# A list scheduler's time model: measured matmul distances and a port lock between VectorE and GpSimd

## The chip, the core and the metric

The kernel runs on one core of one Trainium2 chip. A core has a matrix engine (TensorE, "PE" in the profile; its weight loads are shown as "PEld"), a vector engine (VectorE, "DVE"), an activation engine (ScalarE, "ACT"), a general engine (GpSimd, "POOL") and SyncE ("SP"), whose queue issues all DMAs of this kernel. Each engine works through its own queue in the order in which the program put the instructions there, and waits at an instruction until the semaphores that it needs are set. The metric is the device time of one execution in microseconds, as the median of several runs.

## What is computed

Two layers of a streaming encoder on 2048 frames of width 1024, in float32. Each layer has a gated linear attention (4 heads, chunks of 64) and a differential softmax attention (4 heads, two maps each), one input projection and one output projection:

```
for l in range(DEPTH):
    mod = c_act @ w_ada[l] + b_ada[l]
    shift, scale, gate = jnp.split(mod, 3, axis=-1)
    h = rms_norm(x, norm_g[l]) * (1.0 + scale[:, None]) + shift[:, None]
    proj = h @ w_in[l]
    gq, gk, gv, glr, gz, dq, dk, dv, dz = split_columns(proj)
    gqkv = jax.nn.silu(causal_depthwise_conv(jnp.concatenate([gq, gk, gv], axis=-1), conv_w[l]))
    ...
    o_gla = gla_branch(gq, gk, gv, glr, gz, w_gk[l], b_gk[l], gla_norm_g[l])
    ...
    o_diff = diff_branch(dq, dk, dv, dz, qn_g[l], kn_g[l], lam, lam_init, diff_norm_g[l])
    y = jnp.concatenate([o_gla, o_diff], axis=-1).astype(x.dtype) @ w_out[l]
    x = x + gate[:, None] * y
```

## The kernel before

**Tiling.** The frames are taken in 4 blocks of 512 (`UT`), for each of 2 layers. For a block, `prep_gen` loads x, normalises and transposes it to `hhi` and `hlo`, the high and low halves of h^T in a rounded float32 type (F32R). `dense_gen` runs the input projection as items of 512 columns: three matmuls of 512 columns for each pair of 128-row tiles (high x high, high x low, low x high), summed in the accumulators `acc` (4 banks of PSUM, the matmul's output memory). `gla_gen` works the linear attention (`uT`: convolved values before their transposes; `E`, `vN`: keys and values; `Sn`: states). `head_evac` and `qk_gen` bring one softmax head's queries and keys to `qh`, `ql` and `Kt` (`rq`: a reciprocal root, made by GpSimd's pow; `qk`: rows scaled by it). `attn_gen` takes a head in 4 query tiles: scores into `sc`, VectorE's running minimum into `s`, ScalarE's exp, VectorE's combination of the two maps with the factor `r`, transposes into `tp`, a copy `aT` by ScalarE, and the product with V into `po`; `z` is the gated result, `oT` its transpose. `out_gen` splits `oT` into `oh` and `ol` and runs the output projection.

**Weights.** `weights` (line 552) loads a weight tile. At the first block of a layer (u = 0) it loads the raw tile, ScalarE rounds the high half, GpSimd subtracts for the low half (line 562), and both are written to DRAM (`wd`); the later blocks load the split tile from there. GpSimd's subtractions are therefore all in the first block's pass of each layer, and in the output projection's first pass of each layer.

**What sets the order.** The generators run as streams and record every operation in `Program.ops`, with its dependences and a cost in ns (`cost`). Then `order` plays the program: it keeps for each engine the time at which it is free, for each operation the time at which its inputs and its buffer are there (with fixed latencies `LAT` between engines), and picks again and again the engine that can start first, giving it, of the operations that are ready, the one recorded first. Matmuls count double where the modelled clock is cold. The result is one list, and `issue` (line 277) emits the instructions in that order, so that it fixes each engine's queue, SP's with the DMAs among them. All instructions come from one line of `issue`, which is why the profile puts L284 on every group; groups are told apart by their tiles. On the chip, semaphores hold the order of dependences; the modelled times have no effect there.

**Lines that matter.** `cost`, line 160: for TensorE a fixed 110 ns for a transpose; for a matmul n columns over a rate, with a lower bound from the 107 ns of a weight load or from 216 ns, plus 3. For GpSimd 300 + 165 n ns for pow and 100 + 2.2 n otherwise. For VectorE 0.52 ns a column for copies and `tensor_scalar` on SBUF operands (SBUF is the on-chip memory of the engines), 1.042 otherwise, plus fixed parts. `order`: line 243 takes the ready operation, the last `else` (line 258) advances the free time of VectorE, GpSimd and, outside of table loads, ScalarE.

Of the kernel before, what the change touches and what calls it, by code (L numbers as in the profile page):

```python
# [20 lines left out]
P = 128  # L21
# [4 lines left out]
CH = 64  # L26
# [91 lines left out]
class Program:  # L118
# [40 lines left out]
    @staticmethod  # L159
    def cost(e, method, args, kw, out):  # L160
        n = math.prod(out.shape[1:])
        if e == "S":
            return math.prod(out.shape) * 4 / 360.0
        if e == "T":
            if method == "transpose":
                return 110
            rate = {F32R: 2.4, BF16: 2.4, F32: 0.6}[args[2].dt]
            if rate == 0.6 and args[1].shape[1] < P:
                return max(n / rate * args[1].shape[1] / P, 78)
            return max(n / rate, 107 * args[1].shape[1] / P if rate == 2.4 else 216) + 3  # L170
        ins = [a for a in list(args[1:]) + list(kw.values()) if isinstance(a, View) and a is not kw.get("accum_out")]
        scalars = sum(math.prod(a.shape[1:]) == 1 for a in ins) if n > 1 else 0
        psum = any(a.buf.psum for a in ins)
        if method == "tensor_reduce":
            n = math.prod(ins[0].shape[1:])
        if e == "A":
            return 0.834 * n + (52 if psum else 93) + 93 * (scalars + ("accum_out" in kw))
        if e == "G":
            return 300 + 165 * n if kw.get("op") == ALU.pow else 100 + 2.2 * n
        fast = method in ("tensor_copy", "tensor_scalar") and not psum  # L180
        return (0.52 if fast else 1.042) * n + 68 + 61 * scalars

    @staticmethod
    def table(op):
# [3 lines left out]
    def order(self):  # L188
        ops, N = self.ops, len(self.ops)
        left, uses, turn = {}, [], {}  # L190
        for o in ops:
            for b in o[6]:
                if b not in left:
                    left[b] = 0
                    turn.setdefault((b.pool, b.tag), []).append(b)
                left[b] += 1
        place = {b: k for q in turn.values() for k, b in enumerate(q)}
        nxt = dict.fromkeys(turn, 0)
        slots = {t: [{} for _ in range(q[0].bufs or q[0].pool.bufs)] for t, q in turn.items()}
        blocked = {t: [] for t in turn}  # L200
        slot, used = {}, {}
        succ = [[] for _ in range(N)]
        nd = [len(o[4]) for o in ops]
        for i, o in enumerate(ops):
            for j in o[4]:
                succ[j].append(i)
        ready = [0.0] * N
        free = dict.fromkeys(self.engines, 0.0)
        dma = 0.0
        pend = {e: [] for e in free}  # L210
        avail = {e: [] for e in free}
        todo = [i for i in range(N) if nd[i] == 0]
        table, flight = None, [-1e4] * 8
        work, win = {}, 3413
        res = []
        while len(res) < N:
            while todo:
                now, todo = sorted(todo), []
                for i in now:
                    e, bufs = ops[i][0], ops[i][6]  # L220
                    for b in bufs:
                        t = (b.pool, b.tag)
                        if b not in slot and (place[b] != nxt[t] or not slots[t]):
                            blocked[t].append(i)
                            break
                    else:
                        for b in bufs:
                            if b not in slot:
                                t = (b.pool, b.tag)
                                slot[b] = min(slots[t], key=lambda u: max(u.values(), default=0.0))  # L230
                                slots[t].remove(slot[b])
                                used[b] = {}
                                nxt[t] += 1
                                todo += blocked[t]
                                blocked[t] = []
                            for e2, x in slot[b].items():
                                ready[i] = max(ready[i], x + (self.LAT[e2][e] if e != e2 or e == "S" else 0))
                        heapq.heappush(pend[e], (ready[i], i))
            t, e = min((free[e] if avail[e] else max(free[e], pend[e][0][0]), e)
                       for e in free if avail[e] or pend[e])  # L240
            while pend[e] and pend[e][0][0] <= t:
                heapq.heappush(avail[e], heapq.heappop(pend[e])[1])
            i = heapq.heappop(avail[e])
            if e == "S":
                free[e] = t + 475
                dma = end = max(dma, t + 1150, flight[-8] + 2000) + ops[i][5]
                flight.append(end)
            elif e == "A" and self.table(ops[i]) not in (None, table):
                table = self.table(ops[i])
                free[e] = end = t + ops[i][5] + 1283  # L250
            elif e == "T":
                w = int(t / win)
                warm = work.get(w - 1, 0.0) > 0.5 * win
                free[e] = end = t + ops[i][5] * (1 if warm else 2)
                if ops[i][1] == "transpose" or ops[i][2][2].shape[-1] > 1:
                    for v in range(w, int(end / win) + 1):
                        work[v] = work.get(v, 0.0) + min(end, (v + 1) * win) - max(t, v * win)
            else:
                free[e] = end = t + ops[i][5]
            res.append(i)  # L260
            for j in succ[i]:
                ready[j] = max(ready[j], end + self.LAT[e][ops[j][0]])
                nd[j] -= 1
                if nd[j] == 0:
                    todo.append(j)
            for b in ops[i][6]:
                used[b][e] = max(used[b].get(e, 0.0), end)
                left[b] -= 1
                if left[b] == 0:
                    t_ = (b.pool, b.tag)  # L270
                    slots[t_].append(used[b])
                    todo += blocked[t_]
                    blocked[t_] = []
        self.span = max(free.values()) / 1e3
        return res
# [12 lines left out]
def trunk_kernel(ctx, tc, x, c, w_ada, b_ada, norm_g, w_in, conv_w, w_gk, b_gk, gla_norm_g,  # L288
# [226 lines left out]
    def pe(cost, wait=0.0):  # L515
        return ("pe", cost, wait)
# [614 lines left out]
    def dense_stream():  # L1131
        order = (0, 4, 1, 2, 5, 3, 6)
        prev = None
        for l in range(L):
            for u in range(NU):
                yield need("h", l * NU + u, lag=2.0)
                if prev:
                    yield from out_gen(*prev)
                yield from dense_gen(l, u, (0, 4, 1, 5, 2, 3, 6) if u == 0 else order)
                prev = (l, u)  # L1140
        yield from out_gen(*prev)
# [47 lines left out]
```

## Time and profile before

| | us |
|---|---|
| median of 3 runs | 2660.28 (2659.81 to 2660.94) |
| the profiled execution | 2664.22 |
| its span, first to last instruction | 2662.5 |
| TensorE busy | 2573.6 |
| VectorE busy | 1768.3 |
| ScalarE busy | 1207.0 |
| GpSimd busy | 625.3 |

The profiled execution is a single one and has a time of its own, 1.7 us longer than its span. A row of the groups reads: line, engine, operation, output tile <- input tiles, shapes, count, then busy us, mean ns of one, then the idle time of the engine before such an instruction and who ended it. A row of the waits reads: who waited, for whom, total us, number of times, longest us. A row of a timeline reads: start us, length us, engine, line, operation, tiles, shape, count, and in brackets the idle time before it. A row of the chain that ended last reads: start us, length us, engine and tile, count. A matmul's busy time is longer than its distance to the next one, since they are pipelined.

### The profile page before, as it was taken

The numbers are of one execution on the slowest core, as the hardware profiler recorded it, in microseconds if no ns is written. First come the engines' busy times: TensorE is split into PE (matmuls) and PEld (weight loads), VectorE is DVE, ScalarE is ACT, GpSimd is POOL, SyncE is SP. The second block draws the span as 40 slices with busy tenths as digits, with TensorE's granted clock in tenths as the row PEclk, the third lists the DMA queues.
The fourth block names the chain that finished last, engine by engine and source line by source line (L and its number), as shares of the span: only waits on it lengthen the run. The fifth ranks groups of instructions, "written<-read, shape, count | busy, mean of one in ns | idle before, by whom it ended". The sixth has DMA issues, their size and how long they took to land. (4 is left out here: it accounts for less than half of the span.)

```text
span 2662.5 us, 41105 instructions
## 1 busy us (share of the span) xinstructions
PE 2573.6 (97%) x13987; PEld 2070.3 (78%) x13987; DVE 1768.3 (66%) x5104; ACT 1207.0 (45%) x2592; POOL 625.3 (23%) x852
## 2 busy tenths in 40 slices
PE   7999899999999999999999989999999999999997
PEld 4777678877888778887777767887788877888886
DVE  4778757873767837676738764667637786387764
ACT  3555524453444533444634563344614456154442
POOL 2455411121010210102154554111121111210111
PEclk9999999999999999999999999999999999999998
DMA  8766586446552465334277656443374433734242
GB/s 278 243 229 240 205 295 198 160 154 213 170 186 96 151 206 171 139 131 136 83 263 250 230 202 244 163 175 139 124 262 151 150 130 112 265 121 153 91 139 103
DMA packets 201613, 476.12 MB, mean 179 GB/s; under 512 B 20735, under 2 KB 78269, under 8 KB 201405
## 3 DMA queue, kind: packets, MB, share of 16 engines
q1 hardware_dynamic: 201404, 473.50, 52.1%
q8 instruction: 111, 1.82, 0.3%
q14 instruction: 98, 0.79, 0.1%
HBM read 362.29 MB, written 111.15 MB: 178 GB/s over the span
## 5 line engine op out<-in xcount | busy, mean ns | idle before, releaser
L284 PE MATMUL acc<-w,hhi 128*128 128x512 f32 x2560 | 844.5, 405 | 5.9 <-DMA w<-wd 2.8
L284 PEld LDWEIGHTS acc<-w,hhi 128*128 128x128 f32 x2560 | 462.5, 189 | 106.0 <-issue 13.1
L284 PE MATMUL acc<-w,hlo 128*128 128x512 f32 x1280 | 507.4, 398 | 0.0
L284 ACT ACTIVATE s<-s,mx 128x512 f32<-128x512 f32 (+15 forms) x256 | 308.0, 1204 | 342.7 <-DVE s L284 341.3
L284 PE MATMUL acc<-hhi,w 128*128 128x512 f32 x1024 | 373.6, 406 | 1.2 <-DVE z L284 0.5
L284 PE MATMUL acc<-w,oh 128*128 128x512 f32 x1024 | 335.8, 403 | 8.6 <-DVE t L284 4.7
L284 DVE TENSOR_SCALAR_CACHE_REDUCE s<-sc,mx 64x64 f32<-64x64 f32 (+5 forms) x640 | 307.5, 485 | 43.6 <-PE sc L284 25.2
L284 PEld LDWEIGHTS acc<-w,hlo 128*128 128x128 f32 x1280 | 241.2, 188 | 51.1 <-issue 2.0
L284 POOL MEMSET s<- 64x64 f32 x256 | 39.0, 154 | 1027.3 <-DVE s L284 463.7
L284 POOL TENSOR_TENSOR w<-raw,w 128x512 fp32r<-128x512 f32 x144 | 195.0, 1364 | 194.1 <-ACT w L284 171.3
L284 PEld LDWEIGHTS acc<-w,oh 128*128 128x128 f32 x1024 | 191.2, 191 | 53.7 <-DVE t L284 8.5
L284 PEld LDWEIGHTS acc<-hhi,w 128*128 128x128 f32 x1024 | 192.5, 188 | 41.7 <-issue 1.2
L284 ACT COPY aT<-tp 128x512 f32<-128x512 f32 (+2 forms) x320 | 162.7, 520 | 115.5 <-PE tp L284 111.7
L284 PE MATMUL po<-Vj,aT 128*128 128x128 f32 x1536 | 205.2, 277 | 4.9 <-ACT aT L284 4.8
L284 PE MATMUL acc<-w,ol 128*128 128x512 f32 x512 | 202.9, 400 | 0.9 <-DVE ol L284 0.7
L284 PE MATMUL acc<-hlo,w 128*128 128x512 f32 x512 | 203.0, 396 | 0.0
L284 DVE TENSOR_SCALAR_CACHE_REDUCE s<-sc 128x512 f32<-128x512 f32 (+4 forms) x256 | 158.5, 623 | 66.9 <-PE sc L284 62.5
L284 PEld LDWEIGHTS po<-Vj,aT 128*128 128x128 f32 x1536 | 191.6, 193 | 14.6 <-ACT aT L284 9.1
L284 DVE SCALAR_TENSOR_TENSOR s<-s,r 128x512 f32<-128x512 f32 (+2 forms) x320 | 200.6, 676 | 2.9
L284 DVE TENSOR_TENSOR ol<-oT,oh 128x512 fp32r<-128x512 f32 x128 | 105.2, 828 | 120.2 <-ACT oh L284 108.7
L284 PE MATMUL tp<-ident,s 128*128 128x128 f32 x1088 | 172.5, 274 | 11.8 <-DVE s L284 9.4
L284 POOL TENSOR_TENSOR rq<-qss,mhalf 128x4 f32<-128x4 f32 x128 | 128.9, 1026 | 192.8 <-DVE qss L284 192.4
(167 smaller groups left out, 4209.2 us busy)
## 6 DMA issues: line engine op xcount, KB each, us to landing
w<-wd SPq DMA_DIRECT2D x432, 512.0 KB, 3.6
wd<-w SPq DMA_DIRECT2D x144, 512.0 KB, 3.4
raw<-in_w_in_dram SPq DMA_DIRECT2D x112, 256.0 KB, 4.3
Kj<-kd SPq DMA_DIRECT2D x48, 512.0 KB, 5.0
wr<-in_w_ada_dram SPq DMA_DIRECT2D x128, 128.0 KB, 3.2
kd<-Kt SPq DMA_DIRECT2D x24, 512.0 KB, 2.8
Vj<-vd SPq DMA_DIRECT2D x48, 256.0 KB, 4.1
xt<-in_x_dram SPq DMA_DIRECT2D x16, 512.0 KB, 3.8
```

The source lines that it names most:

```text
L284: getattr(self.engines[e], method)(*[real(a) for a in args], **{k: real(v) for k, v in kw.items()})
```

## The change

Only the two functions that model time are changed, with a new one beside them; no operation is added or removed, and the buffers are the same. In `cost`, a matmul with F32R (or BF16) operands takes 0.4512 ns a column, at least 112 ns for a full weight load and with no constant; F32 matmuls get 7 ns in place of 3; narrow F32 matmuls on 64 rows take 1.4 times as long. The new `paired` says which operations use the ports that VectorE and GpSimd share: four methods, with no operand in PSUM, all of GpSimd's and those of VectorE with more than one element a row. In `order`, a time `ports` holds until when these ports are taken: an engine whose next operation is paired takes the first ready operation that isn't, if there is one; else it starts when the ports come free. GpSimd's `memset` isn't paired, its pow (a `tensor_tensor`) is, for its whole cost.

```diff
             if rate == 0.6 and args[1].shape[1] < P:
-                return max(n / rate * args[1].shape[1] / P, 78)
-            return max(n / rate, 107 * args[1].shape[1] / P if rate == 2.4 else 216) + 3
+                return max(n / rate * args[1].shape[1] / P, 78) * (1.4 if args[1].shape[0] == CH else 1)
+            if rate == 2.4:
+                return max(0.4512 * n, 112 * args[1].shape[1] / P)
+            return max(n / rate, 216) + 7
...
+    @staticmethod
+    def paired(op):
+
+        e, method, args, kw = op[:4]
+        if e not in "VG" or method not in ("tensor_tensor", "scalar_tensor_tensor", "tensor_copy", "tensor_scalar"):
+            return False
+        ins = [a for a in list(args[1:]) + list(kw.values()) if isinstance(a, View) and a is not kw.get("accum_out")]
+        return not any(a.buf.psum for a in ins) and (e == "G" or math.prod(args[0].shape[1:]) > 1)
...
+        paired, ports = [self.paired(o) for o in ops], 0.0
...
             i = heapq.heappop(avail[e])
+            if paired[i] and ports > t:
+                later = [i]
+                while paired[i] and avail[e]:
+                    i = heapq.heappop(avail[e])
+                    later.append(i)
+                if paired[i]:
+                    i = later[0]
+                    t = ports
+                later.remove(i)
+                for j in later:
+                    heapq.heappush(avail[e], j)
...
             else:
                 free[e] = end = t + ops[i][5]
+                if paired[i]:
+                    ports = end
```

## The prediction

> **What bounds the kernel now.** I read the profile's page first, then the busy time by stage, then what TensorE waited for in each stage, because the change touches nothing but the order in which the instructions stand on their queues: it can win or lose only where an engine waits.
>
> ```profile
> span 2662.5 us, 41105 instructions
> PE 2573.6 (97%) x13987; PEld 2070.3 (78%) x13987; DVE 1768.3 (66%) x5104; ACT 1207.0 (45%) x2592; POOL 625.3 (23%) x852
> ...
> 0.00:60.00 60.00, 42.22 (x276) 28.22 (x277) 26.79 (x102) 18.92 (x38) 12.51 (x22) 0.97 0.86 279
> 60.00:400.00 340.00, 314.91 (x1561) 240.93 (x1559) 242.60 (x638) 163.79 (x391) 149.29 (x162) 0.99 0.72 243
> 400.00:1330.00 930.00, 923.14 (x5194) 753.48 (x5193) 644.68 (x1914) 433.64 (x891) 147.51 (x246) 1.00 0.47 157
> 1330.00:1600.00 270.00, 251.29 (x1278) 197.84 (x1276) 183.07 (x500) 132.82 (x332) 136.90 (x152) 0.98 0.69 233
> 1600.00:1940.00 340.00, 333.79 (x1743) 264.85 (x1742) 205.29 (x604) 149.16 (x329) 73.56 (x103) 1.00 0.49 173
> 1940.00:2600.00 660.00, 659.28 (x3694) 544.59 (x3693) 439.01 (x1291) 292.09 (x583) 98.23 (x160) 1.00 0.45 156
> 2600.00:2662.50 62.50, 48.99 (x254) 40.37 (x252) 26.87 (x58) 16.53 (x31) 7.28 (x8) 0.89 0.29 101
> ```
>
> The columns after the length of a stretch are busy time and count of PE, PEld, DVE, ACT and POOL, then the granted TensorE clock. TensorE is busy 97% of the span; all its idle time is 2662.5 - 2573.6 = 88.9 us. That is the whole purse, since no matmul is removed. It is not spread evenly: 17.8 us lie before 60 us, 25.1 in 60 to 400, 6.9 in the next 930, 18.7 in 1330 to 1600, 6.2 up to 1940, 0.7 in the 660 us after that, and 13.5 at the tail. The two costly middle stretches are those where GpSimd is busy 44% (149.29 of 340) and 51% (136.90 of 270) of the time, against 15% (98.23 of 660) in the calm late stretch: there each layer meets its weights first and GpSimd computes the low halves (line 562). What TensorE waits for in these two stretches (60 to 400 first, then 1330 to 1600; total, times, longest):
>
> ```profile
> PE tp L284 <- DVE uT L284: 3.8, 2, 2.5
> PE tp L284 <- DVE s L284: 2.9, 5, 1.0
> PE sc L284 <- DVE Kt L284: 2.9, 4, 0.9
> ...
> PE sc L284 <- DVE hhi L284: 1.9, 1, 1.9
> PE sc L284 <- DVE am L284: 1.8, 1, 1.8
> PE tp L284 <- DVE r L284: 1.5, 1, 1.5
> ```
>
> ```profile
> PE tp L284 <- DVE s L284: 3.5, 6, 1.7
> PE tp L284 <- DVE uT L284: 3.2, 2, 2.4
> PE sc L284 <- DVE xss L284: 3.0, 1, 3.0
> PE acc L284 <- ACT oh L284: 2.0, 2, 1.8
> ...
> PE sc L284 <- DVE Kt L284: 1.5, 3, 0.7
> ...
> PE tp L284 <- DVE z L284: 1.2, 1, 1.2
> ```
>
> Nearly all are waits for VectorE. Here is one of them, in the order DVE, POOL, PE, and the stage after it:
>
> ```profile
> 1428.65 1.53 DVE L284 TENSOR_SCALAR t<-ub,vec 128x512 f32<-128x512 f32 x1
> 1430.10 1.50 DVE L284 SCALAR_TENSOR_TENSOR am<-wr,cact,am 128x256 f32<-128x256 f32 x1
> 1431.53 1.75 DVE L284 SCALAR_TENSOR_TENSOR uT<-t,t 128x512 f32<-128x512 f32 x1
> ...
> 1428.50 4.22 POOL L284 TENSOR_TENSOR w<-raw,w 128x512 fp32r<-128x512 f32 x3 [5.55 <-ACT w L284]
> ...
> 1433.42 1.09 PE L284 MATMUL tp<-ident,uT 128*128 128x128 f32 x4 [2.44 <-DVE uT L284]
> ...
> 1433.20:1436.60 3.40, 3.18 (x10) 0.50 0.99 311
> ```
>
> Three GpSimd subtractions stand back to back for 4.22 us, and three VectorE instructions beside them take 1.5 us or more each, one per subtraction (4.22 / 3 = 1.4 us); the transposes of uT, which the order had put there, then hold TensorE for 2.44 us, and the next 3.40 us run at half clock (0.50), another 1.7 us lost. The stretching is a matter of this neighbourhood, as the same instruction (ol) shows in 60 to 400 and in 1940 to 2600 (min/median/max ns):
>
> ```profile
> L284 DVE TENSOR_TENSOR ol<-oT,oh x16: 680/1026/1774, 121.1 to 338.5; 128x512 fp32r<-128x512 f32 x16
> ...
> L284 DVE TENSOR_TENSOR ol<-oT,oh x27: 681/692/843, 1941.0 to 2592.2; 128x512 fp32r<-128x512 f32 x27
> ```
>
> **The change part by part.** Nothing is added to or taken from the work. Four edits alter the list scheduler's times, hence its order; the DMAs on SP's queue are the same ones too, and may stand in another order.
>
> First, the distance of a 512-column matmul goes from 216.3 ns (512 / 2.4 + 3) to 231.0 (0.4512 x 512). The trace's own value, from a piece of the chain without a wait:
>
> ```profile
> 1934.39 48.77 PE acc L284 x212
> ```
>
> 48.77 / 212 = 230.0 ns, so the new figure is right and the old one was 6.8% short. The small F32 edits (219 to 223 ns, and 1.4 times for 64-row operands) point the same way. What this does: a matmul that needs a result of another engine is placed behind the filler that fits into the modelled latency. With TensorE thought 6.8% too fast, too much filler was placed, and on the chip this is a cushion: the result is there early. The edit takes that cushion away. Cost: the chain between a query tile's last score and its first transpose has
>
> ```profile
> L284 DVE SCALAR_TENSOR_TENSOR s<-s,r 128x512 f32<-128x512 f32 x224 | 158.6, 752 | 2.2
> ...
> L284 DVE TENSOR_SCALAR_CACHE_REDUCE s<-sc,mx 128x512 f32<-128x512 f32 x192 | 143.2, 748 | 24.1 <-PE sc L284 19.1 <-DVE r L284 0.3
> ...
> L284 ACT ACTIVATE s<-s,mx 128x2048 f32<-128x2048 f32 x16 | 32.0, 2002 | 25.0 <-DVE s L284 25.0
> ```
>
> 0.75 + 2.0 + 0.75 = 3.5 us at the longest, of which 6.8% is 0.24 us. There are 2 layers x 4 blocks x 4 heads x 4 tiles = 128 tiles, so the worst case is 128 x 0.24 = 31 us, if every tile stood just in time. The best case is 0: in 1940 to 2600 all waits together are 0.7 us, so most tiles stand far from the edge. I take 3 us, a tenth, nearest to that row.
>
> Second, a port lock: a VectorE instruction on SBUF operands and a GpSimd tensor instruction never overlap in the model. In 60 to 400 and 1330 to 1600 this makes modelled VectorE results later, as they are on the chip, so the PE queue gets its transposes and scores behind more dense matmuls. Which waits can go? Those where dense work lies next to the waiting matmul: uT, s, Kt, r in the first stretch (3.8 + 2.9 + 2.9 + 1.5 = 11.1) and s, uT, Kt, z in the second (3.5 + 3.2 + 1.5 + 1.2 = 9.4), 20.5 us in all. The others stand where a block ends and the next begins (hhi, am, xss, oh): nothing is left there to fill with, and I count nothing. The bounds are 0 (fillers run out, because the accumulators that the next dense item needs are emptied by the same late VectorE) and 20.5 (as in the calm stretch). Nothing between is nearer, so I take half, 10.2 us. With the uT wait at 1433 its half-clock stage goes as well: 1.7 us (bounds 0 and 8.5, for the five such stages of these two stretches, of which these are the first and the last):
>
> ```profile
> 276.10:279.50 3.40, 3.08 (x8) 0.50 0.90 287
> ...
> 1597.00:1600.40 3.40, 3.40 (x14) 0.51 0.04 16
> ```
>
> The Trainium skill's page "TensorE: Matmul & The Clock Gate", section "What's actually happening", has the array fall back to half clock after at least one idle window of about 3.4 us. In the rows above a gap of 2.44 us was enough, so the rows decide; by the page alone this term would be 0 and the sum 1.7 us higher.
>
> What the chip does is not changed: the port conflicts stay, and the order merely stops waiting on them. The model also overcharges them. It lets a pow on GpSimd hold the ports for its whole 960 ns (300 + 165 x 4), while in the trace, POOL first, then DVE:
>
> ```profile
> 2514.36 2.96 POOL L284 TENSOR_TENSOR rq<-qss,mhalf 128x4 f32<-128x4 f32 x3 [4.69 <-DVE qss L284]
> ...
> 2515.51 0.42 DVE L284 TENSOR_TENSOR qk<-rw,rq 128x256 f32<-128x256 f32 x1
> ...
> 2516.91 0.42 DVE L284 TENSOR_TENSOR qk<-rw,rq 128x256 f32<-128x256 f32 x1
> ```
>
> two products run through under three back-to-back pows at 0.42 us, unstretched. In the model the four products of a head now come up to four pows later, about 4 us, and the head's scores with them, 32 times. TensorE has dense work to run meanwhile, so I price this at nothing; without that cover, at the block ends, it would be up to 4 us each, 8 x 4 = 32 us, and since VectorE takes waiting PSUM readers first, it may as well gain. Both ends go into the range. The Trainium skill's page "SBUF — State Buffer", section "Who interferes with whom", says that a VectorE instruction with two SBUF inputs contends with a GpSimd instruction that reads SBUF, and that the second to issue blocks until the first ends. The uT rows agree (1.75 us under a subtraction); the qk rows do not (0.42 us under a pow). If the rule held for pow too, the model would be exact there, and the term would still be nothing.
>
> Third, when VectorE's next instruction is paired and the ports are taken, the model lets it take a later unpaired one. This is a reordering of VectorE's queue within a microsecond or so, behind TensorE; priced at nothing, cover as above.
>
> The start (17.8 us idle) is set by loads and by the first chain of VectorE results, and the tail (13.5 us) by the last head; the edits don't shorten either. Sum, against the profiled execution's own 2664.2 us (span 2662.5): 2664.2 - 10.2 - 1.7 + 3 = 2655.3. The median of the runs, 2660.3, lies 3.9 below the profiled one, so 2651.4, or **2651 us**, 0.35% faster.
>
> **The rivals.** A difference under 0.2%, about 5 us, can't be told from none here. *No net change:* the GpSimd-dense stretches are held by the ports and by accumulators that VectorE must empty, and a wait taken from a transpose comes back on a dense matmul two microseconds later. For: VectorE and GpSimd together are busy 392 of 340 us in 60 to 400. Against: VectorE alone leaves 97 us of it free. Then 2664.2 - 0 - 0 + 0 less 3.9: 2660.
>
> *The whole purse:* all 20.5 us of these waits go, three half-clock stages with them (5.1), and no cushion is lost: 2664.2 - 25.6 - 3.9 = 2635. For: the late stretch, with the same kind of work and GpSimd at 15%, waits 0.7 us in 660. Against: there the dense work is longer, beside longer attention.
>
> *Slower, the cushion:* with TensorE's distances exact, any latency that the model has short (an exp with a table load, a stretched VectorE instruction on a 1-element operand, which the lock leaves out) stops TensorE, and half of the tiles show it: 128 / 2 x 0.24 = 15.4 us, with only half of the expected gain (5) in return: 2660.3 + 15.4 - 5 = 2671. For: in 400 to 1330 and 1600 to 1940 the queue already touches the edge in places:
>
> ```profile
> PE tp L284 <- DVE s L284: 1.2, 4, 0.4
> ...
> PE tp L284 <- DVE s L284: 1.9, 4, 0.5
> ```
>
> Against: only 3.1 us. It decides once these two rows together rise above some 15 us.
>
> **How the numbers follow.** The forecast has 0.41 (its own range 2640 to 2656), no net change 0.21, the whole purse 0.11, the cushion or the overcharged pows 0.27. Faster by over 0.2% (under 2655): 0.37 of the forecast, 0.11, and 0.01 of no change: 0.49. Slower (over 2665.6): 0.25 of the cushion and 0.03 of no change: 0.28. The rest, 0.23, is within. The range reaches from a little below the whole purse to a little above the cushion, 2630 to 2677; the 31 and 32 us ends would be 2690 and more and get the tail.
>
> **What would show it.** Right: the waits on uT, s and Kt in the first pass of each layer fall from 20.5 to about 10 us; the half-clock stage near 1433 is gone; ol and the conv instructions still stretch next to GpSimd's subtractions, with TensorE busy over them; 400 to 1330 and 1600 to 2600 idle by 14 to 20 us. Wrong: the same waits with other names (dense matmuls on ub or Vt, scores on Kt), or new waits on s and aT in the calm stretches, or a longer tail, because another head ends last; any single gap over 2.4 us costs its half-clock stage besides.

## The result and the profile after

The changed kernel takes 2691.5 us (median of 4 runs, 2684.7 to 2696.3) against 2660.1 (2657.6 to 2660.9): 31 us slower where 9 us faster were forecast. Beside the experiments the kernel before had medians of 2663.6 to 2664.8, and against these the loss is 27 to 28 us; the ratio of the change to the kernel before is 1.0104, with a 95% interval of 1.0091 to 1.0118, in line with the latter. The four runs lie 11.6 us apart, roughly in step with the granted clock: 2684.7 us at 0.994, 2696.3 us at 0.990. The profiled execution is the slowest of them. First its page, then the busy time by stage (after the length: busy time and count of PE, PEld, DVE, ACT, POOL, then the granted clock):

```profile
span 2694.6 us, 41079 instructions
PE 2595.7 (96%) x13987; PEld 2076.2 (77%) x13987; DVE 1776.7 (66%) x5104; ACT 1208.3 (45%) x2592; POOL 637.4 (24%) x852
```

```profile
0.00:60.00 60.00, 39.94 (x269) 26.36 (x270) 28.22 (x102) 18.91 (x38) 11.90 (x22) 0.99 0.87 284
60.00:400.00 340.00, 315.55 (x1542) 243.15 (x1540) 234.83 (x622) 162.03 (x386) 154.17 (x160) 0.97 0.71 239
400.00:1330.00 930.00, 916.13 (x5093) 740.38 (x5092) 639.58 (x1898) 421.86 (x876) 150.16 (x245) 1.00 0.46 156
1330.00:1600.00 270.00, 257.15 (x1293) 201.32 (x1292) 180.82 (x484) 128.50 (x312) 126.86 (x139) 0.98 0.66 226
1600.00:1940.00 340.00, 331.06 (x1750) 262.03 (x1749) 216.10 (x637) 157.07 (x354) 81.90 (x115) 0.99 0.49 171
1940.00:2600.00 660.00, 655.16 (x3633) 536.05 (x3632) 427.38 (x1239) 286.47 (x573) 104.17 (x160) 1.00 0.45 156
2600.00:2694.60 94.60, 80.74 (x418) 66.95 (x417) 49.73 (x125) 33.48 (x56) 8.21 (x12) 0.91 0.33 112
```

TensorE does the same 13987 matmuls, and is idle 98.9 us instead of 88.9. In the two stretches with GpSimd's subtractions it is idle 24.5 and 12.9 us (before: 25.1 and 18.7), in the three calm ones 13.9 + 8.9 + 4.8 = 27.6 us (before 13.8); the stages themselves lie up to some 25 us later than before. What TensorE waits for in 60 to 400 now:

```profile
PE sc L309 <- DVE Kt L309: 6.2, 5, 1.9
PE sc L309 <- DVE nlam L309: 4.9, 1, 4.9
PE tp L309 <- DVE s L309: 4.5, 2, 2.9
...
PE po L309 <- ACT aT L309: 2.7, 5, 0.8
```

uT (3.8 us before) is gone; Kt and s (2.9 us each before) have grown. The wait on nlam ends at 59.5 us, so it lies in the start; it was 2.1 us before. Idle time explains 10 of the 32 us by which the span grew. The mean granted clock explains some 8 more:

```profile
core 0: 2694.6 us, clock 0.990
```

0.010 x 2694.6 = 27 us against 0.007 x 2662.5 = 19. The other 14 us are left for stops that no idle time of TensorE shows. Here is one that shows only in part, from the timeline of the changed kernel (ACT, then PEld, then PE):

```profile
1184.31 0.57 ACT L309 COPY ub<-acc 128x512 f32<-128x512 f32 x1
...
1184.92 0.30 PEld L309 LDWEIGHTS acc<-w,hhi 128*128 128x128 f32 x2 [0.71 <-ACT ub L309]
...
1184.05 0.47 PE L309 MATMUL acc<-w,hhi 128*128 128x512 f32 x1
...
1184.93 0.74 PE L309 MATMUL acc<-w,hhi 128*128 128x512 f32 x2 [0.40 <-ACT ub L309]
```

ScalarE empties an accumulator until 1184.88, and the matmul that is to overwrite it starts at 1184.93. It stands 0.88 us behind the one before it, where 0.23 is its distance: 0.65 us are lost, but only 0.40 of them are idle time, because the record of a matmul is longer than its distance. A stop under some 0.2 us shows no idle time at all. How much time goes this way can be estimated from the distances. Take each distance between the starts of two successive matmuls at full clock, and subtract the median distance of the same two kinds of matmul in the trace before. What is left over, beyond the idle time, adds up to 146 us before and 159 us after, 12 us more, close to the 14.

The weight loads have shorter records and show more of it. All waits of the weight loads on five kinds of late work, first before, then after (who waited, for whom: total us, times, longest):

```profile
PEld po L284 <- ACT aT L284: 17.5, 29, 3.4
PEld tp L284 <- DVE s L284: 9.4, 21, 1.4
PEld sc L284 <- DVE Kt L284: 9.2, 11, 1.4
...
PEld sc L284 <- DVE s L284: 7.9, 26, 0.7
PEld acc L284 <- ACT ub L284: 5.4, 13, 1.1
```

```profile
PEld po L309 <- ACT aT L309: 24.1, 43, 3.4
PEld sc L309 <- DVE Kt L309: 16.7, 12, 2.3
PEld tp L309 <- DVE s L309: 15.8, 31, 3.4
PEld sc L309 <- DVE s L309: 15.0, 39, 1.2
PEld acc L309 <- ACT ub L309: 10.1, 21, 1.3
```

The five make 49.4 us before and 81.7 after. They are picked: all waits of the weight loads for a named engine make 146.9 us before and 173.4 after. Such a wait is also not time lost one for one: with the lock alone (e2_lock_only below), the same five make 66.2 us at an unchanged time. Two of the five, sc on s and acc on ub, are not results but buffers: a PSUM bank that TensorE wants and that VectorE or ScalarE has not yet emptied.

The loss does not sit in one place; six of the eight blocks add to it. The end of each block's output projection on TensorE, from the two traces:

| layer, block | before, us | after, us | loss in this block, us |
|---|---|---|---|
| 0, 0 | 343.9 | 346.5 | 2.6 |
| 0, 1 | 651.0 | 664.3 | 10.7 |
| 0, 2 | 984.1 | 1000.7 | 3.3 |
| 0, 3 | 1363.6 | 1380.3 | 0.1 |
| 1, 0 | 1647.8 | 1671.6 | 7.1 |
| 1, 1 | 1954.2 | 1976.9 | -1.1 |
| 1, 2 | 2286.6 | 2312.7 | 3.4 |
| 1, 3 | 2656.4 | 2688.5 | 6.0 |

### The profile page after: what moved, and what is told of

The parts are those of the page before. It is cut to its first block, busy times and chain, and to the rows that moved or that the text cites. A ratio compares the mean times of both kernels' runs of the same rounds, so it can differ in the third digit from the quotient of the medians.

```text
span 2694.6 us, 41079 instructions
## 1 busy us (share of the span) xinstructions
PE 2595.7 (96%) x13987; PEld 2076.2 (77%) x13987; DVE 1776.7 (66%) x5104; ACT 1208.3 (45%) x2592; POOL 637.4 (24%) x852
## 5 line engine op out<-in xcount | busy, mean ns | idle before, releaser
L309 ACT ACTIVATE s<-s,mx 128x128 f32<-128x128 f32 (+15 forms) x256 | 308.1, 1204 | 346.2 <-DVE s L309 343.3
L309 POOL TENSOR_TENSOR w<-raw,w 128x512 fp32r<-128x512 f32 x144 | 200.5, 1401 | 188.8 <-ACT w L309 168.9
L309 PE MATMUL tp<-ident,s 128*128 128x128 f32 x1088 | 175.5, 276 | 13.5 <-DVE s L309 9.5
```

Of the source, the lines that this page charges most:

```text
L309: getattr(self.engines[e], method)(*[real(a) for a in args], **{k: real(v) for k, v in kw.items()})
```

## The experiments

All kernels compute the same thing with the same instructions; only the modelled times, and so the order, differ. Each was timed beside the kernel before on the same chip. In the diffs, "-" is the changed kernel's line, or that of the kernel named.

### Which edit it is, and how it depends on the distance

`e1_dist_only` takes the lock out of the changed kernel, `e2_lock_only` puts the old matmul times back into it:

```diff
-        paired, ports = [self.paired(o) for o in ops], 0.0
+        paired, ports = [False] * N, 0.0
```

> The new matmul distances (231.0 ns for 512 columns) without the port lock. Cushion theory (exact distances take away the time that results had in reserve): most of the 31 us loss is here, 2682 to 2695. Lock theory (the modelled lock, above all pow at full length, puts VectorE's queue in a worse order): 2655 to 2667. Scatter theory (any new order lands some 15 us up or down): no telling, between the two.

> The port lock with the old distances (216.3 ns). Cushion theory: 2650 to 2665, the waits of the first pass of each layer lower than before. Lock theory: 2682 to 2695. Scatter theory: no telling.

`e3_dist_040` and `e4_dist_048` are the first with another distance, as are three later ones, `e8_dist_036`, `e11_dist_0417` and `e12_dist_0435`:

```diff
-                return max(0.4512 * n, 112 * args[1].shape[1] / P)
+                return max(0.4 * n, 112 * args[1].shape[1] / P)
```

> No lock, and TensorE modelled still faster, 0.40 ns a column (204.8 ns for 512, 11% short of the chip's 231). Cushion theory: more reserve than before, so 2645 to 2660, fewer waits on DVE s, Kt and ACT aT. Lock theory: like the run without a lock at exact distances, within 5 us. Scatter theory: off the line through the other rates by 10 us or more.

> No lock, and TensorE modelled slower than it is, 0.48 ns a column (245.8 ns for 512, 6% long). Cushion theory: results come late more often than at 0.4512, 2695 to 2720. Lock theory: like the run at exact distances without a lock, within 5 us. Scatter theory: off the line.

> No lock, TensorE modelled at 0.36 ns a column (184 ns for 512, 20% short). Reserve theory: the gain levels off, since most results are early already, 2645 to 2665. Ratio theory: no bound known; the line through 0.48, 0.4512 and 0.40 would give 2625 to 2640.

> No lock, 0.4167 ns a column (213.4 ns for 512, where the kernel before has 216.3), and the small constants of the change (223 ns for a 128-column F32 matmul, 1.4 times for 64 rows). If the rate is what counts: 2655 to 2668, like the kernel before. If a few other places in the order move the time by some 0.5% either way (scatter): anywhere from 2650 to 2680.

> No lock, 0.435 ns a column (222.7 ns for 512). On the line between 0.40 (ratio 0.9976) and 0.4512 (1.0099) it comes to 1.006, 2680. A step just below the exact distance would show 2658 to 2668; scatter, anywhere from 2655 to 2695.

| kernel | ns a column | lock | median, us | ratio to before | 95% interval |
|---|---|---|---|---|---|
| e8_dist_036 | 0.36 | no | 2680.7 | 1.0064 | 1.0045 to 1.0083 |
| e3_dist_040 | 0.40 | no | 2658.3 | 0.9976 | 0.9967 to 0.9985 |
| e11_dist_0417 | 0.4167 | no | 2664.2 | 1.0000 | 0.9991 to 1.0009 |
| e12_dist_0435 | 0.435 | no | 2678.2 | 1.0056 | 1.0039 to 1.0072 |
| e1_dist_only | 0.4512 | no | 2689.9 | 1.0099 | 1.0083 to 1.0114 |
| e4_dist_048 | 0.48 | no | 2732.4 | 1.0259 | 1.0243 to 1.0276 |
| e2_lock_only | old | yes | 2666.0 | 1.0008 | 0.9999 to 1.0018 |
| the change | 0.4512 | yes | 2691.5 | 1.0104 | 1.0091 to 1.0118 |

The distances alone make the whole loss and the lock alone none. From 0.40 to 0.48 the time rises step by step with the modelled distance, all other things equal. Scatter of orders, the second rival theory of these runs, would hardly put five points on one rising curve, and 0.4167 with the change's small constants, another order than before, gives the time of before. The clock has no part in this loss: the four runs of e1_dist_only have 0.992 to 0.995, as the kernel before has. Its profiled execution is 24.4 us longer than that of before; counted as above, its stops at full clock are 26 us longer, 11 of idle time and 15 that no idle time shows. The exact value, 231 ns for 512 columns, is not a special point on it. At 0.36 the time turns back up. Its trace has single stops on aT of up to 3.6 us, 22.6 us in all, some three times the next; that the model, with so fast a TensorE, runs out of filler there is argued only:

```profile
PE po L309 <- ACT aT L309: 22.6, 15, 3.6
PE tp L309 <- DVE s L309: 7.7, 13, 1.7
```

The lock did move waits. In the stretches at which it was aimed, the lock alone shows (TensorE's waits from 60 to 400 us, then its busy time in the two stretches):

```profile
PE tp L307 <- DVE s L307: 6.6, 8, 1.9
PE po L307 <- ACT aT L307: 3.6, 5, 1.0
PE sc L307 <- DVE Kt L307: 3.3, 4, 1.5
PE tp L307 <- DVE oss L307: 2.4, 1, 2.4
```

```profile
60.00:400.00 340.00, 313.37 (x1540) 240.63 (x1538) 242.56 (x624) 161.78 (x386) 156.38 (x160) 0.98 0.71 239
...
1330.00:1600.00 270.00, 251.34 (x1261) 196.89 (x1261) 179.20 (x485) 124.48 (x317) 135.75 (x149) 0.98 0.68 231
```

The wait on uT is gone here too; s has 6.6 us instead of 2.9, and aT and oss have come up to 3.6 and 2.4. The idle time is 26.6 and 18.7 us, where it was 25.1 and 18.7: the waits changed their names.

### Is it the reserve that the wrong distance gave?

With the old distance TensorE was thought 6.8% too fast, so each result and each emptied bank had more time on the chip than in the model. If this reserve was what counted, it can be given back in another way while the distance stays exact. `e5_scaled` slows the other engines' costs and latencies in the model by the same 1.068; `e6_lat300` and `e7_lat600` lengthen the latency of a result to TensorE; `e10_slot300` that of a released buffer; `e9_lat_slot300` and `e13_both600` both; `e14_all300` both, on every hand-over between two engines. All are edits of e1_dist_only. Here e9_lat_slot300; e6 and e7 have only the last line, e10 only the first three, and the numbers are 300 or 600 as the names say:

```diff
-                                ready[i] = max(ready[i], x + (self.LAT[e2][e] if e != e2 or e == "S" else 0))
+                                more = 300 if e == "T" and e2 in "AVG" else 0
+                                ready[i] = max(ready[i], x + more + (self.LAT[e2][e] if e != e2 or e == "S" else 0))
...
-                ready[j] = max(ready[j], end + self.LAT[e][ops[j][0]])
+                ready[j] = max(ready[j], end + self.LAT[e][ops[j][0]] + (300 if e in "AVG" and ops[j][0] == "T" else 0))
```

e14_all300 widens both conditions, and e5_scaled has another edit:

```diff
-                                more = 300 if e == "T" and e2 in "AVG" else 0
+                                more = 300 if e2 in "AVGT" and e != e2 else 0
...
-                ready[j] = max(ready[j], end + self.LAT[e][ops[j][0]] + (300 if e in "AVG" and ops[j][0] == "T" else 0))
+                ready[j] = max(ready[j], end + self.LAT[e][ops[j][0]] + (300 if e in "AVGT" and e != ops[j][0] else 0))
```

```diff
-        self.ops.append((e, method, args, kw, deps, self.cost(e, method, args, kw, out), {v.buf: 0 for v in views}))
+        slow = 1.068 if e in "AVG" else 1
+        self.ops.append((e, method, args, kw, deps, self.cost(e, method, args, kw, out) * slow, {v.buf: 0 for v in views}))
...
-                ready[j] = max(ready[j], end + self.LAT[e][ops[j][0]])
+                ready[j] = max(ready[j], end + self.LAT[e][ops[j][0]] * (1.068 if e != "S" else 1))
```

> Exact matmul distances, no lock, and every cost of VectorE, ScalarE and GpSimd and every latency of an engine times 1.068 (231.0 / 216.3), so that the speeds stand to each other nearly as before the change. If the order depends on the relative speeds alone (both the reserve and the ratio theory): 2655 to 2668, the loss of 25 us gone. If the exact distance is bad by itself (against transposes and F32 matmuls, whose times are not scaled): 2682 to 2695.

> Exact matmul distances, no lock, own costs; only the latency from VectorE, ScalarE and GpSimd to TensorE is 300 ns longer in the model. Reserve theory (a matmul placed exactly where its operand is due stops TensorE for any small delay): most of the loss comes back, 2655 to 2672. Ratio theory (it is the order of the other queues, of buffers and DMAs, that needs a fast TensorE): 2682 to 2695.

> The same with 600 ns. Reserve theory: at or below the kernel before, 2645 to 2665, and waits on DVE s, Kt and ACT aT down to half. Ratio theory: 2682 to 2700.

> The same with the 300 ns on released buffers alone. Release theory: about half of the loss comes back, 2665 to 2680. Ratio theory: 2682 to 2700.

> Exact matmul distances, no lock, and 300 ns of reserve in the model both on results that VectorE, ScalarE and GpSimd hand to TensorE and on buffers that they release to it (PSUM banks of acc, sc, tp). Release theory (at exact distances TensorE comes to a bank just as it is released, and the run with 300 ns on results alone did not cover that): 2655 to 2672. Ratio theory (the loss lies in the order of the other queues): 2682 to 2700.

> Exact matmul distances, no lock, 600 ns of reserve on results and on released buffers towards TensorE (300 gave 1.0042 against 1.0099 without). Release theory with a larger reserve: 1.000 to 1.003, 2658 to 2668. If what is left lies in the order of the other queues: no better than with 300, 2670 to 2685.

> Exact distances, no lock, 300 ns of reserve on every hand-over between two engines of TensorE, VectorE, ScalarE and GpSimd, results and buffers, so that each link of a chain (score, minimum, exp, combination, transpose) gets one. If the reserve is missing along the chains and not only at their last link: 2655 to 2668. If it is only missing at TensorE: 2670 to 2680, as with 300 there.

| kernel (exact distance, no lock) | median, us | ratio to before | 95% interval |
|---|---|---|---|
| e1_dist_only, no reserve | 2689.9 | 1.0099 | 1.0083 to 1.0114 |
| e6_lat300, results | 2698.4 | 1.0126 | 1.0108 to 1.0145 |
| e7_lat600, results | 2693.4 | 1.0106 | 1.0091 to 1.0121 |
| e10_slot300, buffers | 2686.4 | 1.0087 | 1.0071 to 1.0103 |
| e5_scaled, others slower by 6.8% | 2681.0 | 1.0059 | 1.0040 to 1.0077 |
| e9_lat_slot300, both | 2675.1 | 1.0042 | 1.0025 to 1.0059 |
| e13_both600, both | 2666.3 | 1.0011 | 1.0002 to 1.0020 |
| e14_all300, every hand-over | 2659.7 | 0.9982 | 0.9972 to 0.9993 |

My first form of the theory, that results come late at TensorE, fell: 300 or 600 ns on results alone gave nothing. These two runs and e10_slot300 came out in the range of the ratio theory (the order of the other queues needs a fast TensorE). What speaks against that one is the reserve on both. It took the buffers too: both together give back 0.0057 of 0.0099 with 300 ns and 0.0088 with 600, though each alone gives back nothing that its interval tells from zero. With 300 ns on every hand-over, along the chains between VectorE, ScalarE and GpSimd as well, all of the loss is gone, at the exact distance. e5_scaled, which lengthens costs and results but leaves the latency of released buffers alone, gave back 0.0040.

The stops follow. Counted as above, idle and hidden ones together, they are 226 us before, 252 in e1_dist_only, 250 to 253 in the three runs with a reserve on one side only, 238 in e9_lat_slot300, 231 in e13_both600 and 229 in e14_all300. The weight loads' waits of the five kinds, 80.0 us in e1_dist_only, are 34.6 in e14_all300, and the one on ub is no longer in the list:

```profile
PEld po L310 <- ACT aT L310: 11.4, 17, 1.3
...
PEld sc L310 <- DVE s L310: 9.1, 20, 1.2
PEld sc L310 <- DVE Kt L310: 8.5, 9, 2.6
...
PEld tp L310 <- DVE s L310: 5.6, 18, 0.9
```

So the exact distance does no harm by itself: the 26 us are stops, and they go when the model has a reserve on both kinds of hand-over. That a reserve works on each wait by itself, and not in part through the order of the other queues, is argued; e14_all300 changes those queues too.

### Do both add up, and what does the lock do then?

The first two are e9_lat_slot300 and e13_both600 with the distance at 0.40; the third is the changed kernel with that distance; the last is e14_all300 with the lock put back:

```diff
-                return max(0.4512 * n, 112 * args[1].shape[1] / P)
+                return max(0.4 * n, 112 * args[1].shape[1] / P)
...
-        paired, ports = [False] * N, 0.0
+        paired, ports = [self.paired(o) for o in ops], 0.0
```

> No lock, 0.40 ns a column and 300 ns of reserve on results and buffers towards TensorE. If both give reserve and it adds up: 2645 to 2655, the fastest. If 0.40 already has all the reserve that is of use: 2655 to 2672.

> No lock, 0.40 ns a column and 600 ns of reserve towards TensorE (300 gave 0.9929). If more reserve is still of use: 2638 to 2648. If 0.40 with 300 is near the best: 2645 to 2660. If it is overdone, as 0.36 was: over 2660.

> The change as it is, lock and all, with 0.40 ns a column in place of 0.4512. The lock alone gave 1.0008 at the old distances; if it is idle here too: 2655 to 2664. If the lock and a fast TensorE overdo the reserve, as 0.36 did: 2668 to 2685.

> The change as it is, exact distances and lock, with 300 ns of reserve on every hand-over between two engines (without the lock this gave 0.9982). If the lock is idle once there is reserve: 2655 to 2665. If the lock's overcharge adds to the reserve and overdoes it (as with 0.40 and the lock, 1.0056): 2670 to 2690.

| kernel | ns a column | reserve | lock | median, us | ratio to before | 95% interval |
|---|---|---|---|---|---|---|
| e15_040_both300 | 0.40 | 300 ns at TensorE | no | 2645.5 | 0.9929 | 0.9914 to 0.9944 |
| e17_040_both600 | 0.40 | 600 ns at TensorE | no | 2638.0 | 0.9901 | 0.9884 to 0.9917 |
| e16_040_lock | 0.40 | none | yes | 2678.6 | 1.0056 | 1.0038 to 1.0073 |
| e18_lock_all300 | 0.4512 | 300 ns everywhere | yes | 2678.1 | 1.0053 | 1.0036 to 1.0070 |

A fast TensorE and a reserve add up: e17_040_both600 is the fastest of all, 1% under the kernel before. Its five waits:

```profile
PEld po L310 <- ACT aT L310: 10.9, 15, 1.4
PEld sc L310 <- DVE s L310: 7.6, 16, 0.9
...
PEld tp L310 <- DVE s L310: 4.5, 7, 1.7
...
PEld sc L310 <- DVE Kt L310: 2.0, 3, 1.0
PEld acc L310 <- ACT ub L310: 1.4, 3, 0.9
```

26.4 us, against 49.4 before and 81.7 after the change; the stops, counted as above, are 201 us against 226 before. Banks (sc on s, acc on ub) fell from 13.3 to 9.0 us, results from 36.1 to 17.4.

With more reserve in the model than the old distance gave, the lock does harm: 1.0056 against 0.9976 at 0.40, 1.0053 against 0.9982 at the exact distance with 300 ns everywhere. In the profiled executions most of this is the clock, first without the lock, then with it (exact distance, 300 ns everywhere):

```profile
core 0: 2659.2 us, clock 0.996
```

```profile
core 0: 2673.9 us, clock 0.990
```

0.004 x 2659.2 = 11 us against 0.010 x 2673.9 = 27, 16 us of clock for 15 us of span. The trace with the lock has 53.8 us of half-clock stages against 24.4 without, the longest of them this one:

```profile
226.20:239.85 13.65, 12.97 (x75) 9.31 (x75) 9.26 (x34) 5.44 (x19) 2.86 (x7) 0.50 0.35 105
```

Stops of TensorE of over 1.2 us, after the first 40 us, are about as many in both (16 with the lock, 17 without), so why the stages last longer stays open. Nor was it tried whether the pow, held for its whole length in the model, does this. The lock takes clock in all four pairs: the median granted clock of the runs is lower by 0.003 at the old and at the exact distance (8 us) and by 0.006 in these two (16 us). So by this estimate the lock was not idle where it left the time as it was: it lost clock there and won about as much elsewhere.

## Why the prediction was wrong

**The distance edit: right mechanism, wrong size.** The prediction said that the old figure was 6.8% short, that this was a cushion, and that the edit takes it away; it priced this at 3 us "a tenth, nearest to that row", with 0 and 31 us as ends. It measured 26 us (1.0099). Three things failed in this step. The row that I took it to be nearest to, 0.7 us of idle time in 1940 to 2600, cannot show stops shorter than a matmul's record; the weight loads' waits would have shown that TensorE already stood at the edge, 49.4 us on five kinds. I priced one chain, score to transpose, while the buffers of sc and acc and the product with V are such hand-overs too, far more than 128. And the 31 us, which the 26 do not reach, were no true upper end: 0.48 ns a column is 13.6% above the old distance, for which the same working gives 128 x 3.5 x 0.136 = 61 us, and the loss there was 2.59%, 69 us.

**The lock: 10.2 us expected, none found.** The step "dense work lies next to the waiting matmul, so half of 20.5 us goes" failed. The waits on uT went as forecast, and s, aT and oss took their place within the same stretches (26.6 and 18.7 us idle with the lock alone, before 25.1 and 18.7). With the exact distance the lock did lower the idle time there, from 44.2 us in e1_dist_only to 37.3. But the half-clock stages grew at the same time (33.0 to 56.8 us in the whole trace), at half clock a matmul counts as busy for longer, and the time did not fall. No net change is what that rival said, and the lower end, 0, was the right one of the two. That the chip's conflicts stay was right: after the change ol takes (min/median/max ns, 60 to 400 us)

```profile
L309 DVE TENSOR_TENSOR ol<-oT,oh x16: 672/685/1781, 127.2 to 342.1; 128x512 fp32r<-128x512 f32 x16
```

up to 1781 ns still. Its median, though, fell from 1026 ns to 685: the new order put fewer of these instructions beside a subtraction.

**The overcharged lock, priced at nothing.** Right at the old distances (1.0008) and at the exact one (1.0104 against 1.0099), wrong in the two pairs with more reserve: some 0.7 to 0.8% in both pairs. The prediction had up to 32 us as its end, and this is 19 to 21. That it is the overcharge which costs them was not tried.

**The half-clock term.** 1.7 us were to be won; the clock lost 8 us more instead. The stage after the uT wait is gone, but new ones follow stops on nlam, Kt (four times), s, z and a DMA of w, of 1.4 to 4.9 us. The sign "any single gap over 2.4 us costs its half-clock stage" does not hold: in the kernel before, the stop of 2.47 us on uT that ends at 120.60 has no such stage after it, while after the change one of 1.36 us on Kt has:

```profile
1419.57 0.33 PE L309 MATMUL sc<-Kt,qh 128*128 128x128 f32 x1 [1.36 <-DVE Kt L309]
...
1421.20:1424.61 3.41, 3.41 (x10) 2.64 (x10) 3.13 (x20) 2.51 (x9) 1.42 (x2) 0.50 1.00 340
```

So the length of one stop does not decide it.

**Start and tail, priced at nothing:** the tail was right (13.5 us idle before, 13.9 after), while before 60 us the change idles 20.1 us instead of 17.8, with the wait on nlam.

**The rival that came true** is the cushion, at 27%, with 2671 us: its mechanism right, its price too low (15 us for the cushion, where 26 were measured), and its sign to look for wrong. It was to show as idle time on s in 400 to 1330 and 1600 to 1940 above 15 us; those two rows went from 3.1 to 4.6 us only, while the loss lay in short stops and in banks.

## What to carry to other kernels

In this kernel a list scheduler with the exact distance left the bottleneck engine no reserve, and it stopped more often. An old wrong constant may be such a reserve in disguise: vary it in steps before it is replaced. A corrected model needs a reserve on both results and buffers handed to that engine; here that won back the loss of 1% (0.9982 to 1.0011 of the time before) and no more. The 1% gain came with 600 ns each on top of a distance left 11% too short. More is not always better: 0.36 ns a column, without other reserve, was slower again.

## What the runs showed that was not expected

Reserve works only when results and buffers both have it: 1.0126 and 1.0087 alone, 1.0042 together, from 1.0099 without. Why 300 ns on results alone is not even a little better was not settled, nor which of the delays (the port conflicts, memory transfers, the clock's stages) uses the reserve up. And TensorE's idle time tells a third of this loss (10 of 32 us). For stops in an engine that is 97% busy, the waits of its weight loads show more, though not one for one; the distances between its matmuls, added up, followed the times best in the kernels without the lock.
